# Two softmaxes per attention step, in a two-layer encoder on one core

## The chip, the cores and the metric

The kernel runs on one core of a Trainium2 chip. The metric is the device time of one execution in microseconds, the median of several runs; less is better.

## What is computed

Two layers, each: a half-weighted SwiGLU feed-forward block, a mixer of three attention branches on one normalised input, and a second feed-forward block; then a final RMSNorm. There are 256 tokens of width 1024, in float32.

```python
y_a = mixer_a(...)   # 8 heads of 64, 2 key heads, q/k norm, rotary: softmax(q k) v
y_b = mixer_b(...)   # 8 heads, window of 128, learned bias, sink logit in the softmax
y_c = mixer_c(...)   # 4 heads: (softmax1 - lam * softmax2) v, bias, then RMSNorm
branches = jnp.einsum('bsnw,nwd->bsnd', ys, w_branch[l])
merged = jnp.sum(sigmoid(gate_logits) * branches, axis=2)
x = x + merged @ w_out[l]
```

## The kernel before

Every product of a weight with an activation is made of three matmuls (`mm3`, lines 320 to 322): high part by high part, high by low, low by high. So each weight chunk of 1 MB is loaded by SP into `raw`, cast by ScalarE to `hi` (line 303) and subtracted by VectorE to `lo` (line 304), each in two halves, two or three chunks ahead of its use. There are three buffers each of `raw`, `hi` and `lo`.

In the mixer the order on TensorE is written out by the program (a manual schedule); on ScalarE and VectorE a scheduler sets the order when the program is built, and each queue then runs strictly in that order. A weight chunk of the projections is 48 matmuls, given out in four pieces of 12; a piece yields a credit of 0.5. After each piece the loop at the end of `mixer` adds the credit and, where it has reached `PACE`, calls `step()`, which puts one attention step onto the queues.

A softmax goes through these stages. `s1`: scores (line 579) into a PSUM bank `sc`, then on VectorE the row maximum (line 631) or the fused bias and minimum (line 646), on ScalarE the two exponentials (line 636 or 648) and, for A and B, the two scalings by the reciprocal sum (line 622), which leave `e`. `s2`: four transpositions on TensorE (line 586) into `pt`, a cast to `pth` on ScalarE (line 588), a subtraction to `ptl` on VectorE (line 589). `s3`: the product with the values (lines 603 and 604) into one of two `halves`, a copy on ScalarE and an addition on VectorE into `y` (lines 609 and 610); each second head also casts its pair (line 613). For a head of C, `s1` is done for both maps, which are then joined, and `s4` transposes the normalised output. `D1`, `D2` and `D3` say how many steps lie between the stages. Within a step `s2` stands first, then `s3`, `s4`, and the scores last.

The first scores need `kas`, the rotated and normalised key in its two parts, which ScalarE (lines 549, 550) and VectorE (lines 551, 552) write after the transposition of `ek` (line 969).

Of the kernel before, what the change touches and what calls it, by code (L numbers as in the profile page):

```python
# [31 lines left out]
NBK = 32  # L32


PACE = 1.25
D1, D2, D3 = 3, 2, 2


ORDER = ["b0", "b1", "g00", "g01", "g02", "k", "c0", "g10", "g11", "c1", "g12", "g03",
# [28 lines left out]
def encoder(ctx: ExitStack, tc: tile.TileContext, a, rope, onehot, out):  # L68
# [21 lines left out]
    def t1(name):  # L90
        return p1.tile([P, S], F32, tag="t1", name=name, bufs=5)
# [490 lines left out]
    def transpose_p(p):  # L582
        pt = bank(acc, "pt")
        for kt in range(2):
            for qt in range(2):
                nc.tensor.transpose(pt[:, kt, cs(qt)], p[:, qt, cs(kt)], ident)
        h, l = t2("pth", F32R), t2("ptl", F32R)
        nc.scalar.copy(out=h, in_=pt)
        nc.vector.tensor_sub(l, pt, f(h))
        return h, l  # L590
# [8 lines left out]
    def pv(pt, v, vi):  # L599
        o = half()  # L600
        h, l = pt
        for kt in range(2):
            nc.tensor.matmul(o, lhsT=v[:, kt, vi], rhs=h[:, kt, :], start=(kt == 0), stop=False)
            nc.tensor.matmul(o, lhsT=v[:, kt, vi], rhs=l[:, kt, :], start=False, stop=(kt == 1))
        return o

    def head_out(o, par, y):
        own, oth = (LOW, UP) if par == 0 else (UP, LOW)
        nc.scalar.copy(out=y[own], in_=o[oth])
        nc.vector.tensor_add(y[own], y[own], o[own])  # L610

    def pair_out(y, pair, yh, yl):
        nc.scalar.copy(out=yh[:, pair, :], in_=y)
        nc.gpsimd.tensor_sub(yl[:, pair, :], y, f(yh[:, pair, :]))

    def ytiles(n):
        return tuple(py.tile([P, 4, S], F32R, tag="y", name=f"y{n}{i}") for i in "hl")
# [6 lines left out]
    def mixer(l):  # L624
        T = {}
# [36 lines left out]
        def soft_c(h, mp):  # L662
            if mp == 0:
                T["suc"] = sm.tile([P, 2, 2], F32, name="suc")
            su = T["suc"]
            sc = scores(T["qc"][h // 2], h % 2, mp, T["kcs"][h // 2], mp)
            e, _ = biased(sc, T["G", B_HEADS + h], 3.0e38, su[:, mp, :])
            if mp == 0:
                T["e0"] = e
                return None  # L670

            e0 = T["e0"]
            ra, es = sm.tile([P, 2], F32, name="ra"), sm.tile([P, 2], F32, name="es")
            nc.vector.reciprocal(out=ra, in_=su[:, 1, :])
            nc.vector.scalar_tensor_tensor(out=ra, in0=ra, scalar=nlam[:, l:l + 1], in1=su[:, 0, :], op0=ALU.mult, op1=ALU.mult)
            for qt in range(2):
                nc.vector.scalar_tensor_tensor(out=e0[:, qt, :], in0=e[:, qt, :], scalar=ra[:, qt:qt + 1], in1=e0[:, qt, :], op0=ALU.mult, op1=ALU.add)
            nc.vector.scalar_tensor_tensor(out=es, in0=su[:, 0, :], scalar=EPS, in1=su[:, 0, :], op0=ALU.mult, op1=ALU.mult)
            return e0, es
# [28 lines left out]
            nc.vector.scalar_tensor_tensor(out=yl[:, h, :], in0=yt, scalar=g, in1=f(yh[:, h, :]), op0=ALU.mult, op1=ALU.subtract)  # L708


        NU = 24
        plan = [[] for _ in range(NU + D1 + D2 + D3 + 1)]

        def ab_unit(u):
            br, h = u // 8, u % 8
            pair, par = h // 2, h % 2

            def s1():
                if h == 0:
                    T["y", br] = ytiles("ab"[br])  # L720
                T["e", u] = (soft_a if br == 0 else soft_b)(h)

            def s2():
                T["pt", u] = transpose_p(T.pop(("e", u)))

            def s3():
                if par == 0:
                    T["yp"] = t1("y")
                o = pv(T.pop(("pt", u)), T["vab"], 2 * br + pair // 2)
                with tc.high_priority():  # L730
                    head_out(o, par, T["yp"])
                if par == 1:
                    pair_out(T["yp"], pair, *T["y", br])

            plan[u + D1 + D2].append((1, s3))
            plan[u + D1].append((0, s2))
            plan[u].append((3, s1))

        def c_unit(h):
            u = 16 + 2 * h  # L740

            def s1(mp):
                if h == 0 and mp == 0:
                    T["yc"] = ytiles("c")
                T["e", u] = soft_c(h, mp)

            def s2():
                e, T["es", u] = T.pop(("e", u))
                T["pt", u] = transpose_p(e)

            def s3():
                T["of", h] = out_c(h, T.pop(("pt", u)), T.pop(("es", u)))

            def s4():
                turn_c(h, T.pop(("of", h)))

            plan[u + D1 + D2 + D3 + 1].append((2, s4))
            plan[u + D1 + D2 + 1].append((1, s3))
            plan[u + D1 + 1].append((0, s2))
            plan[u].append((3, lambda: s1(0)))  # L760
            plan[u + 1].append((3, lambda: s1(1)))

        for u in range(16):
            ab_unit(u)
# [2 lines left out]
        done = [0]  # L767

        def bias_of(s):
            h = s - 8 if s < 16 else B_HEADS + (s - 16) // 2  # L770
            if 8 <= s < 24 and ("G", h) not in T:
                T["G", h] = bias_tile(h)

        def step():
            s = done[0]
            done[0] += 1
            while s == 16 and later:
                later.pop(0)()
            for i in range(s, s + 3):
                bias_of(i)  # L780
            for _, x in sorted(plan[s], key=lambda x: x[0]):
                x()
# [23 lines left out]
        later = []  # L806
# [37 lines left out]
        def branch(i, y, steps):  # L844

            while done[0] < steps:
                step()
            for n in range(2):
                w = weights()
                ps = [bank(wk, "br") for _ in range(2)]  # L850
                if n == 0:
                    products(ps[0], w, y, 0, (0, 1))
                    yield 0.5
                    products(ps[0], w, y, 0, (2,))
                    products(ps[1], w, y, 1, (0,))
                    yield 0.5
                    products(ps[1], w, y, 1, (1,))
                    products(ps[0], w, y, 0, (3,))
                    gated(i, n, 0, ps[0])
                    yield 0.5  # L860
                    products(ps[1], w, y, 1, (2, 3))
                    gated(i, n, 1, ps[1])
                    yield 0.5
                else:
                    for mp in range(2):
                        products(ps[mp], w, y, mp, (0, 1))
                        yield 0.5
                        products(ps[mp], w, y, mp, (2, 3))
                        gated(i, n, mp, ps[mp])
                        yield 0.5  # L870

        def branch_c(y, steps):
            while done[0] < steps:
                step()
            w = weights()
            ps = [bank(wk, "br") for _ in range(2)]
            for mp in range(2):
                products(ps[mp], w, y, mp, range(3))
            while done[0] < len(plan):
                step()  # L880
            w1 = weights(False)
            ps1 = [bank(wk, "br")]
            products(ps1[0], w1, y, 0, range(3))
            products(ps[0], w, y, 0, (3,))
            gated(2, 0, 0, ps[0])
            products(ps1[0], w1, y, 0, (3,))
            products(ps[1], w, y, 1, (3,))
            gated(2, 0, 1, ps[1])
            yield 1.0
            gated(2, 1, 0, ps1[0])  # L890
            ps1.append(bank(wk, "br"))
            products(ps1[1], w1, y, 1, range(4))
            gated(2, 1, 1, ps1[1])
            yield 1.0

        def rest():
            for t in ORDER:
                if t[0] == "g":
                    yield from gate(int(t[1]), int(t[2]))
                elif t[0] == "r":  # L900
                    i = int(t[1])
                    yield from branch(i, T["y", i], 8 + 8 * i + D1 + D2) if i < 2 else branch_c(T["yc"], len(plan) - 2)
                else:
                    yield from fm(keys_c if t[0] == "k" else queries("q" + t[0]))

# [74 lines left out]
            for v, src in parts_v:  # L980
                nc.vector.scalar_tensor_tensor(out=v[:, tt, :, 1, :], in0=src, scalar=r[:, tt:tt + 1], in1=f(v[:, tt, :, 0, :]), op0=ALU.mult, op1=ALU.subtract)

        credit = PACE - 0.5
        for n, more in enumerate(others):
            credit += more
            if n % 2 and later:
                later.pop(0)()
            while done[0] < len(plan) and credit >= PACE:
                credit -= PACE
                step()  # L990

        accs = [bank(acc, "wacc") for _ in range(4)]

# [82 lines left out]
```

## Time and profile before

| | us |
|---|---|
| median of 3 runs | 1198.6 (1197.69 to 1199.04) |
| profiled execution, its own time | 1199.19 |
| its span, first to last instruction | 1197.4 |
| TensorE matmul busy | 1172.3 (98%) |
| VectorE busy | 846.7 (71%) |
| ScalarE busy | 672.2 (56%) |

The shares are means over stages with different limits. The mixers stand at about 200 to 410 us and 790 to 1000 us of the span. TensorE's granted clock was 0.992 of full over the span.

### The profile page before, as it was taken

To read this page: it belongs to the slowest core of one execution; us is meant where nothing else is said; L and a number is where in the kernel's file an instruction comes from. 1 tells how busy PE (TensorE), PEld (TensorE's weight loads), DVE (VectorE), ACT (ScalarE), POOL (GpSimd) and SP (SyncE) were. 2 spreads that over 40 slices of the span, in tenths; PEclk is the share of its full clock that TensorE was granted. 3 is DMA by queue.
4 is the path that set the end of the run, shared out by engine and by line. 5 is a ranking of instruction groups with operands and counts; after the bars stand their busy time and mean duration, and the time that the engine had idled before them with its cause. 6 is when DMAs were issued, how large, how long until landed. Compare 5 with 4: busy or idle time off the path is not lost.

```text
span 1197.4 us, 23190 instructions
## 1 busy us (share of the span) xinstructions
PE 1172.3 (98%) x9748; PEld 1149.4 (96%) x9748; DVE 846.7 (71%) x1145; ACT 672.2 (56%) x1131; POOL 251.7 (21%) x188
## 2 busy tenths in 40 slices
PE   8999999899999999999999999998999999999997
PEld 8999999799999999999999999998999999999996
DVE  5766668878896776666685656697789868656664
ACT  6444346579965554444454444466998556443443
POOL 2221214300011032121241212242000202222221
PEclk9999999999999999999999999998999999999999
DMA  7759665444555556565555565554455446555550
GB/s 258 250 185 307 211 208 175 146 138 130 174 168 170 183 181 206 180 209 190 197 178 185 203 198 190 185 168 141 141 171 164 140 169 201 193 196 178 196 190 36
DMA packets 169365, 218.15 MB, mean 182 GB/s; under 512 B 4303, under 2 KB 147201, under 8 KB 169261
## 3 DMA queue, kind: packets, MB, share of 16 engines
q1 hardware_dynamic: 168652, 215.09, 54.6%
q8 instruction: 76, 1.25, 0.4%
q10 hardware_dynamic: 464, 1.06, 0.2%
q0 software_dynamic: 144, 0.52, 0.1%
q14 instruction: 29, 0.23, 0.1%
HBM read 215.59 MB, written 4.22 MB: 184 GB/s over the span
## 4 chain that ended last, share of the span: by engine, by line
PE 77%; ACT 9%; DVE 8%; issue 4%; POOL 1%; DMA 0%; POOLq 0%; ACTq 0%; DVEq 0%
PE gu L321 13%; PE gu L320 13%; PE gu L322 13%; PE facc L320 4%; PE facc L321 4%; PE facc L322 4%; PE fm L321 3%; PE fm L320 3%; PE fm L322 3%; ACT hi L303 3%; DVE lo L304 3%; PE facc L404 2%; PE facc L403 2%; PE br L320 2%; PE br L321 2%
## 5 line engine op out<-in xcount | busy, mean ns | idle before, releaser
L304 DVE TENSOR_TENSOR lo<-raw,hi 128x1024 fp32r<-128x1024 f32 x390 | 537.5, 1391 | 144.1 <-ACT hi L303 143.2
L303 ACT CAST hi<-raw 128x1024 fp32r<-128x1024 f32 (+1 forms) x394 | 404.5, 1043 | 403.8 <-issue 361.3
L320 PE MATMUL gu<-xgh,hi 128*128 128x256 f32 x1408 | 390.7, 277 | 0.3 <-ACT hi L303 0.3
L322 PE MATMUL gu<-xgh,lo 128*128 128x256 f32 x1408 | 389.3, 276 | 1.6 <-POOL lo L304 0.9
L321 PE MATMUL gu<-xgl,hi 128*128 128x256 f32 x1408 | 390.1, 277 | 0.5 <-DVE xgl L335 0.5
L321 PEld LDWEIGHTS gu<-xgl,hi 128*128 128x128 f32 x1408 | 264.6, 188 | 2.2 <-DVE xgl L335 1.1
L322 PEld LDWEIGHTS gu<-xgh,lo 128*128 128x128 f32 x1408 | 264.4, 188 | 2.0 <-POOL lo L304 1.1
L320 PEld LDWEIGHTS gu<-xgh,hi 128*128 128x128 f32 x1408 | 264.3, 188 | 1.8 <-ACT hi L303 1.3
L320 PE MATMUL fm<-xgh,hi 128*128 128x256 f32 x640 | 181.6, 284 | 0.0
L321 PE MATMUL fm<-xgl,hi 128*128 128x256 f32 x640 | 180.6, 282 | 0.3 <-DVE xgl L335 0.3
L322 PE MATMUL fm<-xgh,lo 128*128 128x256 f32 x640 | 180.0, 281 | 0.0
L480 POOL TENSOR_TENSOR gr<-gr,R 128x512 f32<-128x512 f32 x44 | 76.9, 1748 | 364.7 <-ACT gr L479 364.7
L320 PE MATMUL facc<-hh,hi 128*128 128x256 f32 x480 | 132.5, 276 | 0.0
L321 PE MATMUL facc<-hl,hi 128*128 128x256 f32 x480 | 132.5, 276 | 0.0
L322 PE MATMUL facc<-hh,lo 128*128 128x256 f32 x480 | 132.5, 276 | 0.0
L321 PEld LDWEIGHTS fm<-xgl,hi 128*128 128x128 f32 x640 | 122.4, 191 | 1.3 <-DVE xgl L335 0.7
L322 PEld LDWEIGHTS fm<-xgh,lo 128*128 128x128 f32 x640 | 122.7, 192 | 0.0
L320 PEld LDWEIGHTS fm<-xgh,hi 128*128 128x128 f32 x640 | 122.2, 191 | 0.1
L507 POOL TENSOR_TENSOR hl<-hid,hh 128x512 fp32r<-128x512 f32 x41 | 73.1, 1783 | 145.2 <-ACT hh L506 145.2
L322 PEld LDWEIGHTS facc<-hh,lo 128*128 128x128 f32 x480 | 90.1, 188 | 0.0
L320 PEld LDWEIGHTS facc<-hh,hi 128*128 128x128 f32 x480 | 90.1, 188 | 0.0
L321 PEld LDWEIGHTS facc<-hl,hi 128*128 128x128 f32 x480 | 90.1, 188 | 0.0
(232 smaller groups left out, 1741.8 us busy)
## 6 DMA issues: line engine op xcount, KB each, us to landing
raw<-in_w_ffn_in_dram SPq DMA_DIRECT2D x87, 1024.0 KB, 5.1
raw<-in_w_ffn_out_dram SPq DMA_DIRECT2D x44, 1024.0 KB, 4.9
raw<-in_w_in_dram SPq DMA_DIRECT2D x38, 1024.0 KB, 5.1
raw<-in_w_branch_dram SPq DMA_DIRECT2D x12, 1024.0 KB, 5.1
raw<-in_w_out_dram SPq DMA_DIRECT2D x8, 1024.0 KB, 4.9
G<-skew SPq DMA_DIRECT2D x24, 192.0 KB, 5.3
raw<-in_w_in_dram SPq DMA_DIRECT2D x8, 512.0 KB, 5.1
skew<-vec_d SPq DMA_DIRECT2D x6, 512.0 KB, 8.7
```

The lines of the kernel that those rows point to most:

```text
L303: nc.scalar.copy(out=hi[:, h], in_=raw[:, h])
L304: (eng or nc.vector).tensor_sub(lo[:, h], raw[:, h], f(hi[:, h]))
L320: nc.tensor.matmul(ps, lhsT=hi[:, k, sl], rhs=xh, start=st, stop=False, **chk)
L321: nc.tensor.matmul(ps, lhsT=hi[:, k, sl], rhs=xl, start=False, stop=False, **chk)
L322: nc.tensor.matmul(ps, lhsT=lo[:, k, sl], rhs=xh, start=False, stop=last, **chk)
L403: nc.tensor.matmul(ps, lhsT=xh[:, k, cs(tt)], rhs=w[1][:, k, sl], start=False, stop=False)
L404: nc.tensor.matmul(ps, lhsT=xl[:, k, cs(tt)], rhs=w[0][:, k, sl], start=False, stop=(last and k == 1))
L480: nc.gpsimd.tensor_mul(gr, gr, Rb)
L507: nc.gpsimd.tensor_sub(hl, hid, f(hh))
```

## The change

An attention step now holds two softmaxes: two heads of A or of B, or both maps of a head of C. There are 12 such steps in place of 24, with one step between all stages (`D1, D2, D3` of 1, 1, 1 in place of 3, 2, 2). The pace is a step per 2.6 credits in place of 1.25. The first step comes after four pieces (credit starts at -2.0) in place of after one. The loads of bias tiles `G` look ahead by one such step.

```diff
-PACE = 1.25
-D1, D2, D3 = 3, 2, 2
+LEAD, PACE = 2.0, 2.6
+D1, D2, D3 = 1, 1, 1
...
-        NU = 24
-        plan = [[] for _ in range(NU + D1 + D2 + D3 + 1)]
+        NU = 12
+        plan = [[] for _ in range(NU + D1 + D2 + D3)]
...
-            plan[u + D1 + D2].append((1, s3))
-            plan[u + D1].append((0, s2))
-            plan[u].append((3, s1))
+            s = u // 2
+            plan[s + D1 + D2].append((1, s3))
+            plan[s + D1].append((0, s2))
+            plan[s].append((3, s1))
...
-            plan[u].append((3, lambda: s1(0)))
-            plan[u + 1].append((3, lambda: s1(1)))
+            s = u // 2
+            plan[s + D1 + D2 + D3].append((2, s4))
+            plan[s + D1 + D2].append((1, s3))
+            plan[s + D1].append((0, s2))
+            plan[s].append((3, lambda: s1(0)))
+            plan[s].append((3, lambda: s1(1)))
...
-            while s == 16 and later:
+            while s == 8 and later:
                 later.pop(0)()
-            for i in range(s, s + 3):
+            for i in range(2 * s, 2 * s + 4):
                 bias_of(i)
...
-        credit = PACE - 0.5
+        credit, pace = -LEAD, 0.0
         for n, more in enumerate(others):
             credit += more
             if n % 2 and later:
                 later.pop(0)()
-            while done[0] < len(plan) and credit >= PACE:
-                credit -= PACE
+            while done[0] < len(plan) and credit >= pace:
+                credit -= pace
                 step()
+                pace = PACE
```

TensorE, a step in branch B of the first layer (`fm` is projection work, `sc` the scores). Before:

```order
L322 MATMUL fm<-xgh,lo 128x256
L586 MATMUL pt<-ident,e 128x128 x4
L603 MATMUL halves<-pth,vab 128x256
L604 MATMUL halves<-ptl,vab 128x256
L603 MATMUL halves<-pth,vab 128x256
L604 MATMUL halves<-ptl,vab 128x256
L579 MATMUL sc<-kbs,qb 128x256 x4
L320 MATMUL fm<-xgh,hi 128x256
```

After:

```order
L323 MATMUL fm<-xgh,lo 128x256
L587 MATMUL pt<-ident,e 128x128 x8
L604 MATMUL halves<-pth,vab 128x256
L605 MATMUL halves<-ptl,vab 128x256
L604 MATMUL halves<-pth,vab 128x256
L605 MATMUL halves<-ptl,vab 128x256
```

Each stage now stands twice in a row (8 rows of `halves` in all, then `sc` x8). Between the scores of one step and the transpositions of the next lie 60 matmuls of projection work, or 72 at the first, the fifth and the tenth gap; before, three steps with 24 or 36 between them lay there. The first scores follow 48 matmuls after the transposition of `ek`; before, 12.

ScalarE, the step that issues heads 4 and 5 of A in the first layer. Before, a stretch that holds the same kind of work:

```order
L303 CAST hi<-raw 128x1024 x2
L609 COPY y<-halves 64x256
L588 CAST pth<-pt 128x512
L303 CAST hi<-raw 128x1024 x2
L609 COPY y<-halves 64x256
L636 ACTIVATE e,su<-sc,nb,sA 128x256 x2
L818 ACTIVATE gates_2826<-gates_2826 128x512
L588 CAST pth<-pt 128x512
L622 ACTIVATE e<-e,su 128x256 x2
```

After:

```order
L304 CAST hi<-raw 128x1024 x2
L589 CAST pth<-pt 128x512
L610 COPY y<-halves 64x256
L589 CAST pth<-pt 128x512
L610 COPY y<-halves 64x256
L614 CAST yah<-y 128x256
L304 CAST hi<-raw 128x1024
L637 ACTIVATE e,su<-sc,nb,sA 128x256 x3
L623 ACTIVATE e<-e,su 128x256 x2
L637 ACTIVATE e,su<-sc,nb,sA 128x256
L821 ACTIVATE gates_2826<-gates_2826 128x512
L623 ACTIVATE e<-e,su 128x256 x2
```

The casts of transposed heads, the copies, a weight cast, four exponentials, a gate and four scalings now form one block per step.

VectorE, the step that issues heads 4 and 5 of B in the first layer (`lo` a weight half, `ISA` the fused bias and minimum). After:

```order
L305 TENSOR_TENSOR lo<-raw,hi 128x1024 x2
L800 SCALAR_TENSOR_TENSOR qc<-fm,R 128x512
L305 TENSOR_TENSOR lo<-raw,hi 128x1024
L611 TENSOR_TENSOR y<-y,halves 64x256
L532 TENSOR_TENSOR qc<-qc 64x2x256
L590 TENSOR_TENSOR ptl<-pt,pth 128x512 x2
L611 TENSOR_TENSOR y<-y,halves 64x256
L647 ISA e,nb<-sc,G,nsink 128x256
L647 ISA nb 128x1
```

Three further pairs of `ISA` rows follow, then a `lo`, an addition, a `qc` and the reciprocals of the two sums. Before, never more than two of the fused rows stood between other work of this kind, and each reciprocal had its own place.

## Rows read from the trace of the kernel before

**Rows 1.** The page, busy time of each engine over the span.

```profile
PE 1172.3 (98%) x9748; PEld 1149.4 (96%) x9748; DVE 846.7 (71%) x1145; ACT 672.2 (56%) x1131; POOL 251.7 (21%) x188
```

**Rows 2.** Waits of TensorE: line, awaited; us in total, times, longest.

```profile
PE sc L579 <- ACT kas L550: 8.1, 2, 4.1
PE halves L603 <- DVE y L610: 4.4, 5, 1.7
```

**Rows 3.** Timeline of TensorE, first scores, layer 0: start, us, instruction [idle before].

```profile
230.85 0.36 PE L320 MATMUL fm<-xgh,hi 128*128 128x256 f32 x1
...
236.55 0.58 PE L579 MATMUL sc<-kas,qa 128*128 128x256 f32 x1 [4.06 <-ACT kas L550]
237.38 1.01 PE L579 MATMUL sc<-kas,qa 128*128 128x256 f32 x3 [0.26 <-DVE kas L552]
238.19 0.41 PE L320 MATMUL fm<-xgh,hi 128*128 128x256 f32 x1
...
245.06 0.28 PE L320 MATMUL fm<-xgh,hi 128*128 128x256 f32 x1
```

**Rows 4.** Timeline, same place in layer 1: TensorE, and ScalarE's table load.

```profile
826.84 0.41 PE L320 MATMUL fm<-xgh,hi 128*128 128x256 f32 x1
...
832.92 0.28 PE L320 MATMUL fm<-xgh,hi 128*128 128x256 f32 x1
```

```profile
830.41 1.28 ACT L636 ACT_TABLE_LOAD   x1 [2.72 <-DVE nb L632]
```

**Rows 5.** Windows, the stretch behind the first wait; the clock is the eighth column.

```profile
core 0: us, PE busy (x) PEld busy (x) DVE busy (x) ACT busy (x) POOL busy (x), PEclk, DMA share, GB/s
236.20:243.00 6.80, 6.19 (x27) 5.90 (x28) 5.32 (x10) 3.96 (x9) 0.00 (x0) 0.50 0.42 129
```

**Rows 6.** Windows, a stretch of the attention steps of A and B.

```profile
262.00:302.00 40.00, 38.28 (x327) 37.84 (x326) 34.92 (x77) 37.52 (x88) 2.95 (x4) 1.00 0.42 137
```

**Rows 7.** Timeline, scores of two heads two steps apart, and their scalings.

```profile
266.31 0.64 PE L579 MATMUL sc<-kas,qa 128*128 128x256 f32 x4
...
276.14 0.63 PE L579 MATMUL sc<-kbs,qb 128*128 128x256 f32 x4
```

```profile
274.19 0.91 ACT L622 ACTIVATE e<-e,su 128x256 f32<-128x256 f32 x2
...
286.63 0.91 ACT L622 ACTIVATE e<-e,su 128x256 f32<-128x256 f32 x2
```

**Rows 8.** Timeline of ScalarE, two weight casts in a row.

```profile
261.92 1.99 ACT L303 CAST hi<-raw 128x1024 fp32r<-128x1024 f32 x2
```

**Rows 9.** Groups by line and shape, 225 to 345 us: busy us, mean ns, idle before.

```profile
L304 DVE TENSOR_TENSOR lo<-raw,hi 128x1024 fp32r<-128x1024 f32 x32 | 38.7, 1219 | 5.5 <-ACT hi L303 5.2
L303 ACT CAST hi<-raw 128x1024 fp32r<-128x1024 f32 x32 | 33.0, 1046 | 2.3 <-issue 1.7 <-PE fm L321 0.5
L622 ACT ACTIVATE e<-e,su 128x256 f32<-128x256 f32 x32 | 14.5, 502 | 2.0 <-DVE su L620 1.8
...
L589 DVE TENSOR_TENSOR ptl<-pt,pth 128x512 fp32r<-128x512 f32 x17 | 11.7, 686 | 0.4 <-ACT pth L588 0.2
...
L588 ACT CAST pth<-pt 128x512 fp32r<-128x512 f32 x17 | 9.9, 580 | 0.2
...
L636 ACT ACTIVATE e<-sc,nb,sA 128x256 f32<-128x256 f32 x16 | 8.9, 558 | 3.9 <-DVE nb L632 3.9
...
L646 DVE CUSTOM_DVE_ANT_0 e<-sc,G,nsink 128x256 f32<-128x256 f32 x16 | 7.1, 477 | 0.1
L610 DVE TENSOR_TENSOR y<-y,halves 64x256 f32<-64x256 f32 x16 | 6.7, 417 | 2.9 <-ACT y L609 2.3
...
L609 ACT COPY y<-halves 64x256 f32<-64x256 f32 x16 | 5.9, 367 | 0.4
...
L631 DVE TENSOR_REDUCE nb<-sc 128x2 f32<-128x512 f32 x8 | 5.4, 681 | 0.7 <-PE sc L579 0.7
...
L818 ACT ACTIVATE gates<-gates 128x512 f32<-128x512 f32 x8 | 5.0, 624 | 0.0
...
L550 ACT CAST kcs<-kc 64x256 fp32r<-64x256 f32 x4 | 1.6, 405 | 0.1
...
L658 DVE TENSOR_TENSOR su<-su,es 128x2 f32<-128x2 f32 x8 | 1.2, 155 | 0.7 <-ACT es L657 0.6
```

More of the change, by code (lines that the diff above doesn't have):

```diff
@@ L755, in s4 @@
                 turn_c(h, T.pop(("of", h)))
-            plan[u + D1 + D2 + D3 + 1].append((2, s4))
-            plan[u + D1 + D2 + 1].append((1, s3))
-            plan[u + D1 + 1].append((0, s2))
-            plan[u].append((3, lambda: s1(0)))
-            plan[u + 1].append((3, lambda: s1(1)))
+            s = u // 2
[4 more added lines that the diff above has]
+            plan[s].append((3, lambda: s1(1)))
         for u in range(16):
@@ L901, in rest @@
                     i = int(t[1])
-                    yield from branch(i, T["y", i], 8 + 8 * i + D1 + D2) if i < 2 else branch_c(T["yc"], len(plan) - 2)
+                    yield from branch(i, T["y", i], 4 + 4 * i + D1 + D2) if i < 2 else branch_c(T["yc"], len(plan) - 1)
                 else:
```

## The prediction

> **What bounds the kernel now.** I read the page first: TensorE is busy 1172.3 us [rows 1], so the time is TensorE's work plus its gaps. Then its waits: 8.1 us for `kas` (once per layer, 4.1 each) and 4.4 us for `y` [rows 2]. Then the timeline at the first scores: after 12 matmuls TensorE stands until 236.55, and until 237.38 for the low part of the key [rows 3]. Then the clock: behind that wait a stretch of 6.8 us has a granted clock of 0.50, the 1.2 GHz level [rows 5]. So the wait costs more than its length. Last, the stage of the attention steps: ScalarE is busy 37.5 of 40 us, VectorE 34.9, TensorE 38.3 [rows 6]. In that stage ScalarE has as little spare time as TensorE; that TensorE hardly waits is due to the three steps between scores and transposition.
>
> **The first step, moved behind 48 matmuls: a gain of 12.9.** On ScalarE and VectorE the order up to `kas` is unchanged, so `kas` comes when it came: high part 236.55, low part 237.38 [rows 3]. TensorE now has 48 matmuls from 230.85 on; the rows at full clock start about 0.115 us apart, so they end at 236.4. It waits 0.2 and then 0.7 us, and eight score matmuls are done by about 238.2. Before, the same work (48 projection and 8 score matmuls) was done at 245.06 [rows 3]: 6.9 us gained. In layer 1, done at 826.84 in place of 832.92 [rows 4]: 6.1. This takes in the half clock, which I expect to vanish, as the longest idle stretch there falls from 4.1 to 0.7. Bounds: nothing, if `kas` slid later with the scores; 12.9, as the rows have it. I take 12.9 since the queues ahead of `kas` are the same.
>
> **The chain from scores to transposition: a loss of 25.6.** The window for it shrinks. Two steps of before, which are one step now, take 276.14 - 266.31 = 9.8 us of TensorE [rows 7]. Before, the transposition came three steps after the scores, some 13 us of other work. Now only 60 matmuls lie between, 6.9 us, or 72, 8.3 us. What the chain needs is shown by two heads of before: scores ending at 266.8 were scaled at 275.1 (274.19 + 0.91), 8.3 us later; scores ending at 276.6 at 287.5, 10.9 us [rows 7]. Both exceed 6.9, and now two heads must be through.
>
> How far it exceeds depends on the new order, so I add up the chain from the end of one step's scalings to the next, along the queue rows that follow one another. Operations of one queue start some 0.09 us before the one ahead ends (two casts take 1.99 for 2 x 1.046, [rows 8, 9]). So net: hi 0.95, lo 1.13, ptl 0.6, pth 0.5, y 0.35, maximum 0.6, exponential 0.55 for A and 0.5 for B, scaling 0.41, gate 0.53, fused bias 0.41, key cast 0.42, all from [rows 9]; qc rows of VectorE have the width of ptl, 0.6.
>
> - Gap 3 (heads 4, 5 of A; second order extract): hi 0.95, two lo 2.3, two ptl 1.2, two y 0.7, two maxima 1.2, the bias 0.1, three exponentials 1.65, two scalings 0.8, exponential 0.55, gate 0.53, two scalings 0.8 and hops 0.3: 11.1. TensorE's own step is 9.8, so it stands 1.3.
> - Gap 2 has no value products, 8.9 of TensorE: chain hi, gate, hi, lo, two ptl, two maxima, bias, then as above: 10.4; loss 1.5. In layer 1 the order is better there: 9.6 and 0.7; its gap 3 gives 10.3 and 0.5.
> - Gap 4: eight key casts stand in ScalarE's queue ahead of the exponentials. ScalarE alone: three hi 2.85, two pth 1.0, two y 0.66, seven of the casts and a `y` pair cast 3.35, the last key cast 0.4, then three exponentials, two scalings, exponential, hi, two scalings 4.75; with 0.3 for a reciprocal behind key subtractions: 13.3. Loss 3.5.
> - Gap 5 has 72 matmuls: 11.2 of TensorE against 10.3. No loss, and 0.9 in hand. Gap 6: 10.4, covered by what is in hand.
> - Gap 7 (heads 4, 5 of B; third extract): gate 0.53, hi 0.95, two lo 2.3, qc 0.6, lo 1.13, y 0.35, qc 0.6, two ptl 1.2, y 0.35, four fused 1.65, lo 1.13, addition, qc and reciprocal 0.8, four scalings 1.65, hops 0.2: 13.4. Loss 3.6.
> - Gap 8: hi, gate, hi 2.4, lo 1.13, y 0.35, two ptl 1.2, y 0.35, fused 0.5, then ScalarE 4.9 (exponentials, sink terms, scalings and a hi between them), hops 0.2: 11.1. Loss 1.3.
> - Gap 1: TensorE arrives at 238.2 + 8.3 = 246.5. VectorE's queue: key parts done 238.2, queries of B, a lo and a query until 241.4, two maxima, query parts until 244.0; exponentials 244.2 to 246.4; scalings to 248.3. Both transpositions are 1.6 late. In layer 1 a table load of 1.28 [rows 4] and a gate ahead of the last scaling: 3.2.
> - C has one transposition per step and one new cast: about 8.5 against 9.4, no loss.
>
> Layer 0: 1.6 + 1.5 + 1.3 + 3.5 + 3.6 + 1.3 = 12.8. Layer 1: 3.2 + 0.7 + 0.5 + 3.5 + 3.6 + 1.3 = 12.8. Together 25.6. Bounds: nothing, as the trace of before shows no such wait; above, the head of before with 10.9 us for the chain against 6.9, in each of the 12 gaps of A and B with 60 matmuls: 12 x 4.0 = 48. I take my sums, which lie nearer the lower half, and half to one and a half times them (13 to 38) for the range.
>
> The Trainium skill (Perfetto Trace Analysis, Optimizing Scalar/DVE Operations) says that where Scalar or Vector leave gaps on other engines, breaking work up may let it finish sooner; that speaks against issuing softmaxes by twos. It agrees with the heads of before, whose chains of 8.3 and 10.9 us stayed unseen behind finer steps [rows 7].
>
> **The rest.** The 4.4 us for `y` [rows 2] go: the sums of a step now have the whole of the next one, and TensorE comes later. If they stayed, 4.4 less is gained. On SP the loads of `G` stand by twos, one step (9.8 us) ahead of use; they wait for the fused rows of the step before last, long done. Cost nothing; if SP's queue held up weight loads behind them, it would show as casts waiting. The PSUM banks suffice: the four are two `pt` and two `sc`, each freed a step earlier. The last head's output has 36 matmuls before the third branch in place of 48, 1.4 us less cover per layer; no wait is there now, so nothing, at most 2.8.
>
> **Sum.** -12.9 - 4.4 + 25.6 = +8.3 on the profiled execution's own 1199.2, 1207.5. The median of the runs is 0.6 lower; 1198.6 + 8.3 gives 1207.
>
> **Rivals.**
> 1. Faster: the chains fit. If ScalarE and VectorE run ahead where I have them wait for one another, the waits fall under 10 us, and the time is 1198.6 - 12.9 - 4.4 + 0 to 10 = 1181 to 1191. For it: VectorE has 13% spare. Against it: ScalarE's 94% [rows 6] and the heads of before [rows 7]. It decides at a chain under 9.8 us. With half of my losses, about 13, the time is 1194.
> 2. No change: losses of about 17 cancel the gains, 1196 to 1201.
> 3. The clock falls in the long gaps. The wait of 4.1 us was followed by the half clock [rows 5]; beyond the wait itself it cost about 2.7 us, since 36 matmuls took 6.4 in place of 4.1 [rows 3] and the scores 0.4 more. In gaps 4 and 7 the stretches would be 2 to 3.5 us. If all four bring it down: 1207 + 4 x 2.7 = 1218. The Trainium skill (TensorE: Matmul & The Clock Gate, Part 1: The HAM clock gate (the "warmup" mystery)) has the clock fall to the half level when the array has been idle and come back with activity. By that rule the long gaps would pay so. The trace bears it out at the first scores alone; the 1.7 us wait [rows 2], which lies in the stretch of [rows 6], left the clock at 1.00.
> 4. The change does not move the first scores off the wait: then 1207 + 12.9 = 1220. The orders speak against it.
>
> **Chances.** Forecast (slower, losses 20 to 38) 0.45; the clock rival 0.1; the fourth 0.02; no change 0.1; faster 0.33, of which 0.2 for waits under 10. A change under 0.2% (2.4 us) is about what the runs can't tell from none. Faster 0.33, same 0.10, slower 0.57. The forecast's own range is 1201 to 1219. For 8 in 10 I reach into the faster cases: 1186 to 1219.
>
> **What would show it.** Right: the wait for `kas` under 1 us in each layer, the clock at full level there, and new waits of the transpositions on the scalings (line 622 of before), largest in gaps 4 and 7, at 20 us or more in total. The forecast is wrong if TensorE shows under 13 us of such waits, or if they come behind `y` or weight casts instead.

## The result: slower by 2.8%, and the profile after

| | before | after |
|---|---|---|
| median, us | 1198.64 | 1232.22 (1229.72 to 1235.91) |
| ratio, 95% interval | | 1.0281 [1.0264, 1.0298] |
| profiled execution, its own time | 1199.19 | 1229.72 |
| its span | 1197.4 | 1228.0 |

The sign was forecast, the size was not: 1207 was predicted, with 1219 as the upper end.

The page of the changed kernel, busy time of each engine; it answers to [rows 1]:

```profile
PE 1182.1 (96%) x9748; PEld 1153.7 (94%) x9748; DVE 848.9 (69%) x1145; ACT 673.5 (55%) x1131; POOL 250.1 (20%) x188
```

The instructions of TensorE are the same in number, its busy time is 9.8 us longer, and the span 30.6. So 20.8 us are new gaps. The waits of TensorE that changed (line, awaited: us in total, times, longest), answering to [rows 2]:

```profile
PE halves L604 <- DVE y L611: 27.0, 16, 2.6
PE pt L587 <- ACT e L623: 5.6, 6, 1.2
...
PE sc L580 <- DVE kas L553: 0.9, 2, 0.5
```

Of the kernel before, the wait for the low part of the key, which [rows 2] do not hold:

```profile
PE sc L579 <- DVE kas L552: 0.5, 2, 0.3
```

The reader is to see three things. The wait for `kas` went from 8.1 (and 0.5 for its low part) to 0.9. The new wait on the scalings, from which the prediction drew its whole loss, is only 5.6. And the wait for `y`, which I had struck off, grew from 4.4 to 27.0. Together: -7.7 + 5.6 + 22.6 = +20.5, nearly all of the new gaps.

The first scores of layer 0, timeline of TensorE (start, us, instruction, idle before), answering to [rows 3]:

```profile
236.50 0.38 PE L580 MATMUL sc<-kas,qa 128*128 128x256 f32 x1
237.34 1.10 PE L580 MATMUL sc<-kas,qa 128*128 128x256 f32 x7 [0.45 <-DVE kas L553]
238.28 0.29 PE L321 MATMUL fm<-xgh,hi 128*128 128x256 f32 x1
```

Eight score matmuls are over at 238.28, where 238.2 was forecast, and the granted clock there is 1.00 where it was 0.50 [rows 5]. The columns of the windows are those of [rows 5], here of the changed kernel:

```profile
231.00:238.00 7.00, 6.54 (x55) 6.15 (x54) 6.94 (x13) 5.27 (x11) 0.00 (x0) 1.00 0.89 296
260.20:263.60 3.40, 0.84 (x7) 0.84 (x8) 3.40 (x5) 2.23 (x5) 0.00 (x0) 1.00 0.04 4
263.60:267.00 3.40, 3.40 (x19) 3.40 (x18) 2.18 (x5) 0.71 (x2) 0.74 (x1) 0.52 0.88 301
287.50:294.30 6.80, 5.74 (x27) 5.75 (x28) 6.06 (x18) 5.29 (x17) 0.73 (x1) 0.51 0.61 185
328.50:331.90 3.40, 3.40 (x18) 3.40 (x17) 3.04 (x12) 2.10 (x8) 0.73 (x1) 0.51 0.83 266
854.10:857.50 3.40, 3.31 (x15) 3.09 (x16) 1.99 (x2) 3.28 (x6) 0.00 (x0) 0.52 0.42 147
867.80:871.20 3.40, 3.08 (x14) 3.08 (x15) 2.70 (x6) 0.95 (x3) 0.48 (x1) 0.51 0.66 208
919.00:922.40 3.40, 3.40 (x18) 3.40 (x17) 3.31 (x11) 2.26 (x7) 0.73 (x1) 0.51 0.61 238
```

The half clock left the first scores and came back inside the attention steps: six stretches, 23.8 us in all, where before there were two of 6.8 (a further one at the end of the program stands in both). Five of the six stand at waits for `y`; the one at 854.1 stands behind two waits on the scalings, of 1.2 and 0.9 us. The second row shows what stood ahead of one of them: TensorE busy 0.84 of 3.40 us. By an estimate (half of the 10.2 us more at half speed) the clock is worth 5.1 of the 9.8 by which TensorE's busy time grew; the other 4.7 I have not taken apart.

One step, which issues scores of branch B and holds the value products of heads 6 and 7 of A, shows what the wait for `y` is. Timeline of the changed kernel, rows of the value product (604, 605), its copy (610) and its addition (611):

```profile
301.74 0.36 PE L604 MATMUL halves<-pth,vab 128*128 128x256 f32 x1
...
302.18 0.28 PE L605 MATMUL halves<-ptl,vab 128*128 128x256 f32 x1
302.69 0.37 ACT L610 COPY y<-halves 64x256 f32<-64x256 f32 x1
303.41 0.40 DVE L611 TENSOR_TENSOR y<-y,halves 64x256 f32<-64x256 f32 x1
303.87 0.39 PE L604 MATMUL halves<-pth,vab 128*128 128x256 f32 x1 [1.41 <-DVE y L611]
...
304.65 0.36 ACT L610 COPY y<-halves 64x256 f32<-64x256 f32 x1 [1.60 <-PE halves L605]
```

The product of the first head is issued, read by ScalarE, then by VectorE, and only when that reading is over does the product of the second head begin, though it goes into the other half of `halves`. Nothing stands between the two on TensorE. This happens in each of the 8 steps of A and B of both layers: 16 times, 27.0 us.

### The profile page after: what moved, and what is told of

Read it like the earlier page. It is cut to its first block, busy times and chain, and to the rows that moved or that the text cites. A ratio compares the mean times of both kernels' runs of the same rounds, so it can differ in the third digit from the quotient of the medians.

```text
span 1228.0 us, 23204 instructions
## 1 busy us (share of the span) xinstructions
PE 1182.1 (96%) x9748; PEld 1153.7 (94%) x9748; DVE 848.9 (69%) x1145; ACT 673.5 (55%) x1131; POOL 250.1 (20%) x188
## 3 DMA queue, kind: packets, MB, share of 16 engines
q8 instruction: 76, 1.25, 0.4%
## 4 chain that ended last, share of the span: by engine, by line
PE 75%; DVE 11%; ACT 9%; issue 3%; POOL 1%; DMA 0%; POOLq 0%; ACTq 0%
PE gu L322 13%; PE gu L321 13%; PE gu L323 13%; PE facc L321 4%; DVE lo L305 4%; PE facc L322 4%; PE facc L323 4%; ACT hi L304 3%; PE fm L322 3%; PE fm L321 3%; PE fm L323 3%; PE br L323 2%; PE br L322 2%; PE br L321 2%; PE facc L405 2%
```

## The experiments

Two theories went into the first runs. One (A): the loss is the order of product, reading, product within a step, since `halves` is one tile and is waited for as a whole. The other (B): the loss is the chain from scores to transposition, as predicted, and shows up at whatever stands next. All runs were timed beside the kernel before on the same chip; ratios are to that.

### Both value products ahead of both readings

```diff
-                o = pv(T.pop(("pt", u)), T["vab"], 2 * br + pair // 2)
+                T["o", u] = pv(T.pop(("pt", u)), T["vab"], 2 * br + pair // 2)
+
+            def s3o():
                 with tc.high_priority():
-                    head_out(o, par, T["yp"])
+                    head_out(T.pop(("o", u)), par, T["yp"])
...
             plan[s + D1 + D2].append((1, s3))
+            plan[s + D1 + D2].append((1.5, s3o))
```

> The changed kernel, with both value products of a step issued before the two readings of their halves (copy and addition into y). Theory A (the two halves count as one tile, so the second product of a step waits for the reading of the first): the 27.0 us of TensorE's waits for y go to under 3, the half-clock stretches with them, and what is left is the chain of the softmaxes, whose waits (transposition behind the scalings) grow from 5.6 to between 10 and 25; time 1195 to 1212. Theory B (the readings are late because ScalarE and VectorE are late after the shortened chain, the halves have no part in it): the waits for y stay above 15 us, or pass whole to the transpositions, and the time stays at 1225 to 1236.

Measured: 1207.64 us, ratio 1.0052 [1.0032, 1.0072]. Waits of TensorE in this run, and its timeline in one step:

```profile
PE pt L587 <- ACT e L623: 12.2, 12, 2.8
```

```profile
273.01 0.28 PE L605 MATMUL halves<-ptl,vab 128*128 128x256 f32 x1
273.13 0.28 PE L604 MATMUL halves<-pth,vab 128*128 128x256 f32 x1
```

The second product now starts 0.12 us behind the first, and no wait for `y` is left among the waits. The ratio fell by 0.0229, or 27.5 us, with a single change of order. Theory A holds, though the half-clock stretches fell from 23.8 to 10.2 us and did not go altogether. With the wait for `y` gone, TensorE comes to the transpositions earlier, and the wait on the scalings rises from 5.6 to 12.2: the two waits had covered one another in part.

This run also shows the chain of the prediction by itself, gap by gap (though the readings stand elsewhere in the queues than in the change). Its timeline, transpositions that waited, layer 0:

```profile
249.19 1.75 PE L587 MATMUL pt<-ident,e 128*128 128x128 f32 x8 [0.69 <-ACT e L623]
...
260.61 0.94 PE L587 MATMUL pt<-ident,e 128*128 128x128 f32 x4 [0.92 <-ACT e L623]
...
270.56 0.94 PE L587 MATMUL pt<-ident,e 128*128 128x128 f32 x4 [0.28 <-ACT e L623]
271.87 0.94 PE L587 MATMUL pt<-ident,e 128*128 128x128 f32 x4 [0.37 <-ACT e L623]
...
295.08 0.95 PE L587 MATMUL pt<-ident,e 128*128 128x128 f32 x4 [1.50 <-ACT e L623]
...
317.18 2.11 PE L587 MATMUL pt<-ident,e 128*128 128x128 f32 x8 [2.82 <-ACT e L623]
```

### The late first step alone, in the kernel before

```diff
-        credit = PACE - 0.5
+        credit = PACE - 2.0
```

> The kernel before, with its first step after four pieces in place of one, nothing else. Theory A and B alike: the two waits for the key (8.1 us) and the half clock behind them go, 12.9 us by the rows: 1184 to 1189. Rival (the wait only moves to the next transposition, or the later end of the steps costs it back): 1194 to 1200.

Measured: 1197.25 us, ratio 0.9969 [0.9956, 0.9982]: a gain of 3.7, much less than the 12.9 expected and in the rival's range. Waits of TensorE, then, on its timeline, the waits for `y` that stand ahead of the scores of the seventh head in either layer (with the scores of the second and the seventh head of layer 1), and two windows: behind the second of these waits, and that of [rows 6]:

```profile
PE halves L603 <- DVE y L610: 8.2, 12, 2.0
...
PE sc L579 <- DVE kas L552: 0.9, 2, 0.5
```

```profile
267.17 0.39 PE L603 MATMUL halves<-pth,vab 128*128 128x256 f32 x1 [1.58 <-DVE y L610]
...
829.43 0.63 PE L579 MATMUL sc<-kas,qa 128*128 128x256 f32 x4
...
852.78 0.57 PE L603 MATMUL halves<-pth,vab 128*128 128x256 f32 x1 [1.98 <-DVE y L610]
...
853.79 1.05 PE L579 MATMUL sc<-kas,qa 128*128 128x256 f32 x4
```

```profile
853.40:856.80 3.40, 3.40 (x20) 3.40 (x20) 2.04 (x6) 2.12 (x7) 0.00 (x0) 0.58 0.50 163
262.00:302.00 40.00, 36.67 (x310) 35.63 (x309) 34.74 (x72) 38.76 (x92) 2.23 (x3) 1.00 0.44 145
```

The gain was there and was given back. Counted from the transposition of `ek`, the second head's scores start after 13.9 us in before and 11.4 here (layer 0), 13.1 and 11.2 (layer 1, where the transposition stands at 818.21); 36 projection matmuls more are done by then, 4.1 us. That is 6.6 + 6.0 = 12.6 us gained, against 12.9 predicted. At the seventh head the starts are 35.6 and 35.2, 34.8 and 35.6, so 4.5 + 3.3 = 7.8 is left. The 4.8 lost between are about what the two waits shown (1.6 and 2.0) and the half clock behind the second come to: 3.4 us of it and so, by an estimate, some 1.7 lost. At the end of the stage, at the first `wacc`, 2.9 + 1.0 = 3.9 is left; what took the further 3.9 these views don't show.

### The early first step, in the changed kernel

```diff
-LEAD, PACE = 2.0, 2.6
+LEAD, PACE = 0.5, 2.6
```

> The changed kernel with its first step after one piece, as before. If the late first step gains 12.9 us in the changed kernel too: 1243 to 1248, with waits for the key of about 4 us in each layer. Rival (in the changed kernel the gain is lost again, since the earlier start gives the chains of later steps more time): 1228 to 1238.

Measured: 1239.80 us, ratio 1.0318 [1.0297, 1.0339]. Waits of TensorE:

```profile
PE halves L604 <- DVE y L611: 31.0, 16, 3.0
PE sc L580 <- ACT kas L551: 8.2, 2, 4.1
```

Between the two expectations. The wait for `kas` is back at 8.2, and the late first step is worth 7.6 us in the changed kernel (1239.80 - 1232.22), or 4.4 by the ratios (0.0037), whose intervals just touch. Either way not the 12.9.

### The readings one step later, in the kernel before

The same split of `s3`, with the readings in the next step, and the branch products a step later with them:

```diff
             plan[u + D1 + D2].append((1, s3))
+            plan[u + D1 + D2 + 1].append((1.5, s3o))
...
-                    yield from branch(i, T["y", i], 8 + 8 * i + D1 + D2) if i < 2 else branch_c(T["yc"], len(plan) - 2)
+                    yield from branch(i, T["y", i], 9 + 8 * i + D1 + D2) if i < 2 else branch_c(T["yc"], len(plan) - 2)
```

> The kernel before, with the readings of a head's half moved one step later, behind the next head's value product. Theory A: the 4.4 us of waits for y in the kernel before come from the same shared tile and go: 1192 to 1196. Theory B: the waits stay or move, 1197 to 1203.

Measured: 1200.29 us, ratio 0.9997 [0.9985, 1.0008]. The wait for `y` in this run:

```profile
PE halves L603 <- DVE y L610: 1.7, 6, 0.5
```

It fell from 4.4 to 1.7, as theory A had it, and the time did not follow: 1192 to 1196 was missed. So in the kernel before, the few waits for `y` were not worth their length.

### The readings late, and two steps from scores to transposition

```diff
-LEAD, PACE = 2.0, 2.6
-D1, D2, D3 = 1, 1, 1
+LEAD, PACE = 2.0, 2.5
+D1, D2, D3 = 2, 1, 1
```

This on the first experiment's kernel, and, in a second run, on the changed kernel as it is. The pace goes with it, so that the steps still fit.

> The changed kernel with the readings of both halves behind both products (as in the run with late readings, 1207.6 us), and two steps in place of one between scores and transposition, pace 2.5 so that all steps still end before branch C. If what is left there is the chain from scores to scalings (12.2 us of waits of the transpositions seen): these waits go to under 2 us and the time is 1187 to 1197. Rival (ScalarE's total work in the stage binds, 97% busy in the kernel before with the late first step): the waits move to y or elsewhere and the time is 1198 to 1207.

Measured: 1194.64 us, ratio 0.9942 [0.9925, 0.9959]. Waits of TensorE:

```profile
PE pt L587 <- DVE ptl L590: 4.3, 4, 1.2
PE sc L580 <- DVE nb L647: 3.3, 4, 0.9
PE sc L580 <- ACT e L637: 2.2, 3, 1.1
```

The wait on the scalings is gone. The three that come in its place are for a bank that has not yet been read: with two steps in flight, the ring of four `pt` and `sc` banks seems short, which no run tested. Against the first experiment the gain is 13.0 us (13.2 by the ratios). That is what the longer distance, with its pace, won back there, net of the three new waits (9.8 us together); 25.6 was predicted for the chain.

> The changed kernel with two steps between scores and transposition, pace 2.5, readings as they are in the change. Theory A (the waits for y come from the second product standing right behind the first, whatever the distance of the chain): waits for y of 20 us or more remain, 1215 to 1230. Theory B (they come from ScalarE and VectorE being late after the short chain): waits for y under 10 us, 1190 to 1207.

Measured: 1234.91 us, ratio 1.0285 [1.0257, 1.0313]. The wait for `y`:

```profile
PE halves L604 <- DVE y L611: 35.5, 16, 5.0
```

The same number of steps in flight without the late readings gains nothing: the wait is again 16 times, now 35.5 us. That is theory A's case, with a time above its range. Between these two runs lie 40.3 us, for the order of two lines. The chain is not what bounds the changed kernel.

### The two parts that help, in the kernel before

The second and the fourth experiment together.

> The kernel before with the late first step (1197.3 us, its waits for y had grown from 4.4 to 8.2) and with the readings of a half one step later. If the shared tile took back the gain of the late first step: waits for y under 3 us and 1188 to 1193. Rival (ScalarE, 97% busy in the stage, sets the pace, so a wait removed comes back behind another): 1194 to 1199.

Measured: 1193.23 us, ratio 0.9932 [0.991, 0.9954], the fastest median of the study, and beside the changed kernel (1.0281) 3.4% less. The wait for `y`, and the window of [rows 6] in this run:

```profile
PE halves L603 <- DVE y L610: 6.9, 11, 1.4
```

```profile
262.00:302.00 40.00, 37.61 (x323) 36.90 (x322) 33.98 (x72) 38.38 (x92) 2.23 (x3) 1.00 0.45 147
```

The late readings, worth nothing alone, add 4.4 by the ratios to the late first step; the longest wait for `y` is 1.4 in place of 2.0, and in the attention steps no stretch at the half clock is left. Of the 12.6 us gained at the start, 7.8 are kept. The wait for `y` did not fall under the 3 us of the first case, and the time lies between the two ranges.

This run also says what the merging itself is worth. Single softmaxes with the late first step and the late readings ran at 0.9932; steps of two with the same two parts and two steps of distance, in the run before this, at 0.9942. The intervals overlap, so no gain of the merged steps is shown.

### One step less in the kernel before

```diff
-D1, D2, D3 = 3, 2, 2
+D1, D2, D3 = 2, 2, 2
```

> The kernel before with two steps in place of three between scores and transposition (one softmax per step, 60 matmuls and one step's attention work between them, some 8.3 us). If the number of softmaxes that stand together makes the chain too long: waits of the transpositions under 4 us in all, 1198 to 1204. Rival (the distance alone does it, since single heads took 8.3 and 10.9 us): waits of 8 us or more, 1206 to 1216.

Measured: 1203.02 us, ratio 1.0024 [1.001, 1.0039]. The new wait:

```profile
PE pt L586 <- ACT e L622: 5.0, 6, 1.2
```

So the chain from scores to transposition does reach past two fine steps, and the third step of before is needed; one less costs 2.0 to 2.9 us. The time is in the range of the first case; the wait of 5.0 lies between the two.

### A quarter of the weight casts on GpSimd

What takes the rest of the gain? The windows show ScalarE at 38.4 to 38.8 of 40 us. If its load does it, fewer casts should free it. The same edit was made in the fastest version and in the one with two steps:

```diff
-            nc.scalar.copy(out=hi[:, h], in_=raw[:, h])
+            casts[0] += 1
+            if state.get("attn") and casts[0] % 4 == 0:
+                nc.gpsimd.tensor_copy(out=hi[:, h], in_=raw[:, h])
+            else:
+                nc.scalar.copy(out=hi[:, h], in_=raw[:, h])
```

> The kernel before with the late first step and the late readings (1193.2 us, 6.9 us of waits for y left, ScalarE busy 38.4 of 40 us in the stage), and every fourth weight cast of the stage on GpSimd in place of ScalarE. If ScalarE's load in the stage keeps the rest of the late first step's gain: waits for y under 4 us, 1184 to 1191. Rival (ScalarE's load does not bind, or a cast on GpSimd is so slow that the weights come late): 1192 to 1205, with waits of the products on hi or lo.

Measured: 1194.53 us, ratio 0.9961 [0.9946, 0.9976], no better than without (0.9932 [0.991, 0.9954]). The waits for `y` and for the key, and the casts on GpSimd (group: times | busy us, mean ns | idle before):

```profile
PE halves L607 <- DVE y L614: 5.5, 7, 1.7
PE sc L583 <- DVE kas L556: 2.4, 2, 1.2
```

```profile
L305 POOL CAST hi<-raw 128x1024 fp32r<-128x1024 f32 x20 | 27.1, 1356 | 109.3 <-PE fm L325 76.4 <-issue 32.0 <-POOL rc L700 0.9
```

The wait for `y` fell by 1.4 from the 6.9 of the same kernel without the casts, and the wait for the low part of the key grew from 0.9 to 2.4. The timeline at the first scores, a cast on GpSimd and the subtraction on VectorE that the scores wait for:

```profile
236.59 1.30 POOL L305 CAST hi<-raw 128x1024 fp32r<-128x1024 f32 x1 [10.60 <-PE fm L325]
...
237.00 1.16 DVE L556 TENSOR_TENSOR kas<-ka,kas 64x256 fp32r<-64x256 f32 x1
```

Without the casts on GpSimd this subtraction took 0.42 us. In layer 1 it took 1.16 as well, again while a cast on GpSimd ran. How a cast there would lengthen it no run shows.

> The changed kernel with late readings and two steps to the transposition (1194.6 us), and every fourth weight cast of the stage on GpSimd. If ScalarE's load sets the waits left there (5.5 us of scores behind a bank that the previous softmax still holds, 4.3 of transpositions behind ptl): 1184 to 1191. Rival (the four PSUM banks hold the scores up whatever ScalarE does, or the slow casts cost it back): 1192 to 1205.

Measured: 1195.28 us, ratio 0.9967 [0.9953, 0.9981], also no gain. The bank waits stay:

```profile
PE pt L591 <- DVE ptl L594: 4.9, 4, 1.4
PE sc L584 <- DVE nb L651: 3.7, 4, 1.0
```

Here too the wait for the key grew, to 2.5. So that ScalarE's load keeps the rest of the gain is not shown. ScalarE was busy 85.7 us in place of 92.4 between 240 and 345 us of the first of these runs and the time did not fall, which speaks against it; but with the casts on GpSimd some 1.5 us were lost at the key, so the runs do not rule it out. For the version with two steps the ring of banks stays the candidate. What takes the last 4 to 5 us in the fastest version stays open.

Two tiles of their own for the two halves might do away with the wait for `y` as well. This wasn't tried: the program holds four PSUM tiles of that size for scores and transpositions and three for work beside `halves`, and one of these would have had to be given up for it.

## Why the prediction was right in sign and wrong in size

**The step that failed** is the sentence "The 4.4 us for `y` [rows 2] go: the sums of a step now have the whole of the next one, and TensorE comes later." They grew to 27.0. I thought of the reading of a step's heads against the products of the next step. I did not ask what the second product of the same step waits for. `halves` is one tile of two halves, and the program makes a product into it wait for the reading issued before it, whichever half that reads. In the kernel before, a whole step lay between the reading of one head and the product of the next, so the wait was seldom seen; the 4.4 us in [rows 2] were for the most part its trace (1.7 was left when the readings were moved), and I took them for a late sum. In the change the two stand back to back. The order that stood ahead of the prediction showed it: eight rows of `halves` in a row on TensorE, and on ScalarE copy and cast by turns. The first experiment shows the cause: products first, readings second, and 27.5 us of the loss are gone.

The Trainium skill (PSUM — Partial Sum Buffer, PSUM bank collisions raise a hardware error) says to guard PSUM by its bank and not by address, since two engines that touch one bank on the same partitions at once collide, at separate columns too. The trace agrees in that the product waited 16 times for a reading of other columns of its tile; no run here shows what would happen without the wait. By that rule two halves of a bank are one buffer, and the loss could have been foreseen.

**The first step, -12.9.** Right where it was worked out: eight scores done at 238.28 against 238.2, the clock at 1.00, a gain of 12.6 at the second head of the kernel before with this part alone. Wrong as a gain in the total: 3.7 in the kernel before, 4 to 8 in the changed one. The stage did not keep what TensorE gained at its start. I should have priced what is late next; by the seventh head, with a wait for `y` ahead of it in either layer, 4.8 of it was gone.

**The chain, +25.6.** The mechanism was right, the size twice too large: 12.2 us of waits without the wait for `y`; two steps of distance then won 13.0 us of time, net of new waits. By gap, over both layers, predicted and measured in the first experiment: the first 4.8 and 2.8, the second 2.2 and 0.9, the third 1.8 and 1.0, the fourth 7.0 and none, the fifth none and 3.2, the seventh 7.2 and 4.2, the eighth 2.6 and none. For C, where none was predicted, TensorE waited 0.8. So the seventh is the largest, as forecast. The eight key casts that I charged to the fourth do stand there in the changed kernel, and TensorE waited 0.9 at it in either layer, not 3.5. In the first experiment the new order of ScalarE's queue has three of the eight in the fifth gap of layer 0 (from 282.4 to 286.5), where TensorE waited 1.5; that the wait is theirs is not shown. My sums string all the queue rows that stand between one after another; that this made them high is likely, but no run tested it. In the changed kernel itself 5.6 is left, as the wait for `y` gave the chain time.

**The rivals.** The sign that was to show the forecast wrong, "if TensorE shows under 13 us of such waits, or if they come behind `y`", came in both halves. The third rival, the clock, came true mostly at other places: of the 23.8 us at half speed, 20.4 stand at waits for `y`, and 3.4 behind waits on the scalings at the first gap of layer 1. The Trainium skill (TensorE: Matmul & The Clock Gate, Part 1: The HAM clock gate (the "warmup" mystery)) has an idle array fall to the half level. The trace agrees in that all six stretches stand at waits, but not every wait of such a length was followed by one (see the last section). The Trainium skill's rule on breaking work up (Perfetto Trace Analysis, Optimizing Scalar/DVE Operations), cited in the prediction, agrees with the ratio of 1.0281 only by appearance: steps of two softmaxes, with the readings last and two steps of distance, ran at 0.9942, and the single ones with the same two parts at 0.9932, which the runs can't tell apart. That rule of the Trainium skill also speaks of instructions, on engines that are not saturated; no instruction was made larger by the change, and ScalarE stood at 94% [rows 6].

With the failed step taken out, the first experiment ran at 1207.64, close to the 1207 predicted (by the ratio 6.3 us of loss, where 8.3 were predicted). That is chance in part: by the figures above the chain was some 12.6 us too dear, and the first step 5 to 9 too generous.

## What to carry to other kernels

When steps are merged, go through the new order within one step and ask of each buffer who must have read it before the next write; two halves of one tile were waited for here as one buffer. Where two products share it, issue both before either reading. And a gain at the start of a stage is kept only as far as the later waits allow: look for the next of them, and try the part alone before adding it into a sum.

## What was not expected of the hardware

The half clock did not need a wait as long as the 4.1 us at the first scores. In the second experiment one of 1.98 us was followed by 0.58, in the first one of 2.82 by 0.60, and in the changed kernel waits of 0.9 and 2.6 us close together by 0.52, while the wait of 1.7 in the kernel before left it at 1.00. Its length alone did not decide it. In the changed kernel the wait for `y` at the products of heads 0 and 1 of B was 2.32 us in both layers:

```profile
316.06 0.39 PE L604 MATMUL halves<-pth,vab 128*128 128x256 f32 x1 [2.32 <-DVE y L611]
...
918.57 0.39 PE L604 MATMUL halves<-pth,vab 128*128 128x256 f32 x1 [2.32 <-DVE y L611]
```

```profile
316.10:319.50 3.40, 3.40 (x29) 3.40 (x30) 3.30 (x9) 2.26 (x6) 0.49 (x1) 1.00 0.72 276
```

Behind that of layer 0 the clock stayed at 1.00; behind that of layer 1 it was 0.51 (the window from 919.00 above). So two waits of one length can differ in it, and what a wait costs is read from the window behind it. GpSimd's weight cast took 1.36 us where ScalarE's took 1.05 [rows 9].
